# Second MLP product of an encoder block: all columns of the seven middle row chunks in seven products, 512-column matmuls, weight differences on GpSimd

## The chip, the cores and the metric

The kernel runs on one core of a Trainium2 chip. The metric is the device time of one execution in microseconds, taken as the median of several runs. The engines are TensorE (PE in the profile, its weight loads PEld), VectorE (DVE), ScalarE (ACT), GpSimd (POOL) and SyncE (SP), which issues most DMAs. Sources are written L12 for line 12 of the kernel.

## The reference

One pre-norm transformer layer on 512 tokens of width 2048, all in float32. The attention parts are not touched here. What matters is the end:

```python
x = x + mixed @ w_out[l]
h = rms_norm(x, mlp_norm_g[l])
x = x + jnp.square(jax.nn.relu(h @ w_ff1[l])) @ w_ff2[l]      # d_ff = 8192
return rms_norm(x, final_norm_g)
```

The second MLP product is a 512 x 8192 matrix F (the squared ReLU) times w_ff2, 8192 x 2048.

## The kernel before

Every float32 product is made of three passes in a rounded float32 format: an operand is split into a high part (a cast on ScalarE, L89) and a low part (the difference, on VectorE, L90), and the product takes high x high, high x low and low x high. `split` does this for a tile of 128 x 1024 elements, `unit` loads such a tile of weights and splits it into one of four `hi` and four `lo` buffers (the raw load goes through one of three `raw` buffers).

The rows of w_ff2 are taken in nine chunks: 512, seven times 1024, 512. F comes from the first product, which stores each piece of 256 columns to DRAM (`f_d`) with the row sums and differences s1 to s4 that a Strassen step needs (`s_d`). The second product adds into `SF`, a float32 tile in SBUF (two halves of the tokens, four column groups of 512).

The first chunk is a plain product (`plain`): for each of four column groups, 48 matmuls of 512 columns; ScalarE copies the result into SF. A middle chunk does three quarters of the columns in Strassen form and the last quarter plain. `spair` is one Strassen pair: it takes 512 columns as two halves of 256, and makes seven products (`sprod`, L949 to L951) of 2 x 4 x 3 = 24 matmuls of 256 columns each. The products are, in order, a11, a12, s2, s1, s3, s4 and a22, each against one weight block or one sum of weight blocks. Those weight differences are four VectorE subtractions a pair:

```python
TT(b11, b12, b11, ALU.subtract)
TT(t2, b22, b11, ALU.subtract)
TT(b12, b22, b12, ALU.subtract)
TT(t2, b21, t2, ALU.subtract)
```

After each product the PSUM tile is added into SF by VectorE (`sacc`, through the helper at L187). The weights for this are a copy of w_ff2 packed in units of 256 columns, `w_ff2s`. The plain quarter takes 96 matmuls of 512 columns and four additions into SF.

The operands of chunk c+1, four tiles of F and four of sums, are loaded and split during the plain quarter of chunk c; F alternates between two pools, the sums have one set of buffers. The last chunk (512 rows) is plain again and runs together with the residual sum and the final norm (`f2l`).

The order on each engine and on each DMA queue is not that of the text: a planner orders the instructions by their place in the text and by when it expects their operands and buffers, and every engine then runs its list in order. GpSimd has no work in the second product; elsewhere it adds masks (L437) and sums (L492).

Of the kernel before, what the change touches and what calls it, by code (L numbers as in the profile page):

```python
# [17 lines left out]
P = 128  # L18
# [13 lines left out]
NSP = 3  # L32
# [5 lines left out]
def block_kernel(ctx, tc, x, xT, w_c, w_ckv, w_qkv, w_uqn, w_uqr, w_ukv, rpb, gcols, w_out, w_ff1, w_ff2, w_ff2s, g_fin,  # L38
# [88 lines left out]
    # ---------------------------------------------------------------- input norm, latents  # L127
# [123 lines left out]
    # ---------------------------------------------------------------- neighbourhood projections  # L251
# [30 lines left out]
    def strassen_t(nm, getA, b, m1, tile, v, t2):  # L282
        """v[nh][:, token half] = (A B)^T for 256 columns of B given as four blocks."""
# [122 lines left out]
    # ---------------------------------------------------------------- neighbourhood attention  # L406
# [103 lines left out]
    # ---------------------------------------------------------------- attention operands  # L510
# [69 lines left out]
    # ---------------------------------------------------------------- latent attention  # L580
# [88 lines left out]
    # ---------------------------------------------------------------- output projection  # L669
# [174 lines left out]
    def ff1_pair(i):  # L844
# [10 lines left out]
        nc.scalar.dma_start(out=f_d[c][q], in_=vt)  # L855
        if strassen(c):
# [7 lines left out]
            nc.sync.dma_start(out=s_d[c][q], in_=st)  # L864
# [17 lines left out]

    def load_f(c, q):
        if q == 0:
            F[c] = []
        name = f"fa{c}_{q}"
        if c % 2 == 0:
            t = iot(name)
        else:
            t = [fpool.tile([P, UNIT], F32R, name=f"{name}_{j}", tag=f"f{j}", bufs=4) for j in range(2)]  # L890
        if c == 0:
            raw = raw_unit(f_d[c][q], name)
        else:
            raw = fsp.tile([P, UNIT], F32, name=name + "r", tag="fr", bufs=2)
            nc.sync.dma_start(out=raw, in_=f_d[c][q])
        split(t[0], t[1], raw)
        F[c].append([v.rearrange("p (b n) -> p b n", b=4) for v in t])

    def load_s(c, q):
        if q == 0:  # L900
            SS[c] = []
        raw = fsp.tile([P, UNIT], F32, name=f"sr{c}_{q}", tag="fr", bufs=2)
        nc.sync.dma_start(out=raw, in_=s_d[c][q])
        t = [fsp.tile([P, UNIT], F32R, name=f"fs{c}_{q}_{j}", tag=f"fs{q}{j}", bufs=1) for j in range(2)]
        split(t[0], t[1], raw)
        SS[c].append([v.rearrange("p (b n) -> p b n", b=4) for v in t])
# [6 lines left out]
    nf2 = [0]  # L913

    def f2t(name):
        i = nf2[0] % 8
        nf2[0] += 1
        return mmt(name) if i < 4 else (sct, sct, trt, pvt)[i - 4](name)

    def half(ap):  # L920
        return ap.rearrange("p (b n) -> p b n", b=2)

    def plain(c, n, k0, hook):
        ps = [f2t(f"f2_{c}_{n}_{m}") for m in range(NM)]
        ng = CH[c] // 256
        for g in range(ng):
            u = unit(w_ff2[k0 // 256 + g, n], 2, f"w2_{c}_{n}_{g}")
            hook()
            for j in range(2):
                k = 2 * g + j  # L930
                for m in range(NM):
                    mm3(ps[m], fk(c, k, m), pair(u, j, slice(0, 512)), k == 0, k == 2 * ng - 1)
        for m in range(NM):
            if c == 0:
                nc.scalar.copy(sf(m, n), half(ps[m]))
            else:
                TT(sf(m, n), half(ps[m]), sf(m, n), ALU.add)

    BLK = {"a11": 0, "a21": 1, "a12": 2, "a22": 3, "s1": 0, "s2": 1, "s3": 2, "s4": 3}

    def sprod(ps, c, a, b, first):
        kw = dict(skip_group_check=True)
        src = (F if a[0] == "a" else SS)[c]
        for mm in range(2):
            o = ps[:, mm, :]
            for kk in range(4):
                ah, al = (t[:, BLK[a], mm * P:(mm + 1) * P] for t in src[kk])
                bh, bl = (t[:, kk] for t in b)
                nc.tensor.matmul(o, ah, bh, start=first and kk == 0 and mm == 0, stop=False, **kw)  # L949
                nc.tensor.matmul(o, ah, bl, start=False, stop=False, **kw)  # L950
                nc.tensor.matmul(o, al, bh, start=False, stop=kk == 3, **kw)  # L951

    def sacc(ps, th, nb):
        TT(SF[th][:, nb], ps, SF[th][:, nb], ALU.add)

    def spair(c, j, hook):
        nm = f"{c}_{j}"
        kg = 2 * (c - 1)

        def ld(kh, nh):  # L960
            src = w_ff2s[kg + kh, 2 * j + nh]
            if nh == 0:
                return raw_unit(src, f"sb{kh}0_{nm}")
            b = fsp.tile([P, UNIT], F32, name=f"sb{kh}1_{nm}", tag=f"sb{kh}1", bufs=2)
            nc.sync.dma_start(out=b, in_=src)
            return b

        def opS(k, src):
            u = unit_bufs(f"{k}_{nm}")
            split(u[0], u[1], src)  # L970
            return [t.rearrange("p (k n) -> p k n", k=4) for t in u]

        b11, b21, b12, b22 = ld(0, 0), ld(1, 0), ld(0, 1), ld(1, 1)
        PX, PY, PZ = (half(f2t(f"s{x}{nm}")) for x in "xyz")
        t2 = fsp.tile([P, UNIT], F32, name=f"st2_{nm}", tag="st2", bufs=1)
# [181 lines left out]
```

## Time and profile before

| | |
|---|---|
| median of 3 runs | 2032.79 us (2027.8 to 2033.24) |
| span of the profiled execution, first to last instruction | 2028.5 us |
| TensorE busy | 1999.8 us, 99% of the span |
| VectorE busy | 1530.3 us, 75% |
| ScalarE busy | 991.2 us, 49% |
| GpSimd busy | 63.6 us, 3% |
| DMA moved | 307.66 MB, mean 152 GB/s |
| granted TensorE clock, mean | 0.997 |

The profiled execution has no run time of its own on record beside its span; the median of the runs lies 4.3 us above that span. Matmuls are pipelined, so the length that a matmul shows (0.39 us for 512 columns, 0.28 for 256) is longer than the distance to the next; the distance between starts is what counts. The first product ends and the second begins at 1350 us of the span.

### The profile page before, as it was taken

The numbers are of one execution on the slowest core, as the hardware profiler recorded it, in microseconds if no ns is written. First come the engines' busy times: TensorE is split into PE (matmuls) and PEld (weight loads), VectorE is DVE, ScalarE is ACT, GpSimd is POOL, SyncE is SP. The second block draws the span as 40 slices with busy tenths as digits, with TensorE's granted clock in tenths as the row PEclk, the third lists the DMA queues.
The fourth block names the chain that finished last, engine by engine and source line by source line (L and its number), as shares of the span: only waits on it lengthen the run. The fifth ranks groups of instructions, "written<-read, shape, count | busy, mean of one in ns | idle before, by whom it ended". The sixth has DMA issues, their size and how long they took to land. (4 is left out here: it accounts for less than half of the span.)

```text
span 2028.5 us, 34883 instructions
## 1 busy us (share of the span) xinstructions
PE 1999.8 (99%) x14388; PEld 1876.9 (93%) x14388; DVE 1530.3 (75%) x1927; ACT 991.2 (49%) x1429; POOL 63.6 (3%) x73
## 2 busy tenths in 40 slices
PE   8999999999999999999999999999999999999998
PEld 7999999877887899999999999998999999999996
DVE  8787777777435787777878787757888887878776
ACT  5644454565314565555555555555434344444333
POOL 2000010100000000000000000000000000000000
PEclk9999999999999999999999999999999999999999
DMA  8454454431334344445353444456435354453352
GB/s 278 134 182 164 154 166 131 133 99 53 94 124 156 123 162 153 169 144 184 129 187 138 175 154 159 164 166 211 161 131 178 124 170 152 133 200 127 103 207 94
DMA packets 97999, 307.66 MB, mean 152 GB/s; under 512 B 10800, under 2 KB 16688, under 8 KB 97584
## 3 DMA queue, kind: packets, MB, share of 16 engines
q1 hardware_dynamic: 87136, 274.76, 40.5%
q10 hardware_dynamic: 9936, 29.52, 3.7%
q8 instruction: 113, 1.85, 0.4%
q0 software_dynamic: 768, 1.15, 0.2%
q14 instruction: 46, 0.38, 0.1%
HBM read 254.27 MB, written 52.26 MB: 151 GB/s over the span
## 5 line engine op out<-in xcount | busy, mean ns | idle before, releaser
L187 DVE TENSOR_TENSOR SF<-sx,SF 128x512 f32<-128x512 f32 x84 | 57.6, 686 | 16.2 <-PE sx L951 16.1
L90 DVE TENSOR_TENSOR fs<-sr,fs 128x1024 fp32r<-128x1024 f32 x28 | 34.2, 1223 | 20.4 <-ACT fs L89 20.4
L125 POOL TENSOR_TENSOR stat<-stat,nhalf 128x1 f32<-128x1 f32 (+1 forms) x6 | 4.4, 730 | 1409.2 <-DVE stat L124 1409.2
L89 ACT CAST fs<-sr 128x1024 fp32r<-128x1024 f32 x28 | 28.8, 1049 | 27.0 <-DMA sr<-s_d 23.3
L853 ACT ACTIVATE v<-v 128x512 f32<-128x512 f32 x64 | 40.4, 632 | 2.0
L852 ACT ACTIVATE v<-v 128x512 f32<-128x512 f32 x64 | 40.3, 630 | 1.0
L187 DVE TENSOR_TENSOR b<-b,b 128x1024 f32<-128x1024 f32 x32 | 38.9, 1216 | 0.0
L187 DVE TENSOR_TENSOR SF<-sz,SF 128x512 f32<-128x512 f32 x42 | 28.9, 687 | 11.7 <-PE sz L951 11.7
L949 PE MATMUL sx<-st_0hi,fs 128*128 128x256 f32 x112 | 32.8, 292 | 4.4 <-ACT sb_0hi L89 4.4
L99 PE MATMUL f<-w_0hi,fa 128*128 128x512 f32 x88 | 34.4, 390 | 0.0
L100 PE MATMUL f<-w_0lo,fa 128*128 128x512 f32 x88 | 34.3, 390 | 0.0
L101 PE MATMUL f<-w_0hi,fa 128*128 128x512 f32 x88 | 34.2, 389 | 0.0
L99 PE MATMUL f<-w_1hi,fa 128*128 128x512 f32 x88 | 34.2, 389 | 0.0
L100 PE MATMUL f<-w_1lo,fa 128*128 128x512 f32 x88 | 34.2, 389 | 0.0
L101 PE MATMUL f<-w_1hi,fa 128*128 128x512 f32 x88 | 34.2, 389 | 0.0
L90 DVE TENSOR_TENSOR mpt<-mt,mpt 128x512 fp32r<-128x512 f32 x32 | 22.0, 686 | 14.2 <-ACT mpt L89 14.2
L950 PE MATMUL sx<-st_0lo,fs 128*128 128x256 f32 x112 | 32.5, 291 | 0.0
L951 PE MATMUL sx<-st_0hi,fs 128*128 128x256 f32 x112 | 32.5, 290 | 0.0
L949 PE MATMUL sx<-st_1hi,fs 128*128 128x256 f32 x112 | 31.7, 283 | 0.0
L950 PE MATMUL sx<-st_1lo,fs 128*128 128x256 f32 x112 | 31.7, 283 | 0.0
L951 PE MATMUL sx<-st_1hi,fs 128*128 128x256 f32 x112 | 31.7, 283 | 0.0
L949 PE MATMUL sx<-st_2hi,fs 128*128 128x256 f32 x112 | 31.7, 283 | 0.0
(2952 smaller groups left out, 8954.6 us busy)
## 6 DMA issues: line engine op xcount, KB each, us to landing
b<-in_w_ff_dram SPq DMA_DIRECT2D x64, 512.0 KB, 5.9
sb<-in_w_ff2s_dram SPq DMA_DIRECT2D x42, 512.0 KB, 4.3
f_d<-v ACTq DMA_DIRECT2D x32, 512.0 KB, 7.2
s_d<-sv SPq DMA_DIRECT2D x28, 512.0 KB, 6.9
sr<-s_d SPq DMA_DIRECT2D x28, 512.0 KB, 4.6
nb<-in_w_qkv_dram SPq DMA_DIRECT2D x24, 512.0 KB, 4.6
sb_0r<-in_w_ff2s_dram SPq DMA_DIRECT2D x14, 512.0 KB, 5.2
sb_1r<-in_w_ff2s_dram SPq DMA_DIRECT2D x14, 512.0 KB, 4.6
```

Of the source, the lines that this page charges most:

```text
L89: i = nc.scalar.copy(hi, src)
L90: nc.vector.tensor_tensor(out=lo, in0=src, in1=hi.bitcast(F32), op=ALU.subtract)
L99: nc.tensor.matmul(ps, ah, bh, start=first, stop=False)
L100: nc.tensor.matmul(ps, ah, bl, start=False, stop=False)
L101: nc.tensor.matmul(ps, al, bh, start=False, stop=last)
L125: nc.gpsimd.tensor_tensor(out=dst, in0=dst, in1=nhalf[:, :cnt], op=ALU.pow)
L187: nc.vector.tensor_tensor(out=out, in0=a, in1=b, op=op)
L852: nc.scalar.activation(v[h], v[h], AF.Relu)
L853: nc.scalar.activation(v[h], v[h], AF.Square)
L949: nc.tensor.matmul(o, ah, bh, start=first and kk == 0 and mm == 0, stop=False, **kw)
L950: nc.tensor.matmul(o, ah, bl, start=False, stop=False, **kw)
L951: nc.tensor.matmul(o, al, bh, start=False, stop=kk == 3, **kw)
```

## The change

The seven middle chunks are done in Strassen form over all columns. A pair now takes 1024 columns as two halves of 512, so a chunk is two pairs, each product is 24 matmuls of 512 columns, and the plain quarter and the packed copy `w_ff2s` go. The weight blocks are two units of 1024 elements each, with loads of their own; a product splits them one unit at a time into the same four hi/lo buffers. The differences (now eight of 1024 elements a pair) are issued on GpSimd. The products accumulate in PSUM tiles of two banks (`ps_w`, four of them), and an addition into SF covers 1024 elements. F and its sums are stored to DRAM by block, so that one load brings one operand of a chunk; the seven operands of the next chunk are refilled one at a time, each after its last product in the second pair, into the single buffer it had (`load_op`; the buffers are those that held the first product's operands, pool `ops1`, which stays open). The operands of the first middle chunk are loaded ahead of the plain first chunk. The tail's residual tiles and last weights use operand buffers too.

```diff
-NSP = 3
...
+    def raw_unit(src, name, k=0):
+        raw = wp.tile([P, UNIT], F32, name=name + "r", tag="raw", bufs=3)
+        if k:
+            raw = raw.rearrange("p (k n) -> p k n", k=k)
...
-    f_d = [[tc.dram_tile([P, UNIT], F32, name=f"f_d{c}_{q}") for q in range(CH[c] // 256)] for c in range(NC_)]
-    s_d = [[tc.dram_tile([P, UNIT], F32, name=f"s_d{c}_{q}") for q in range(CH[c] // 256)] for c in range(NC_)]
+    f_d, s_d = ([tc.dram_tile([P, 4, CH[c] // 256, 256], F32, name=f"{t}_d{c}") for c in range(NC_)] for t in "fs")
...
-        nc.scalar.dma_start(out=f_d[c][q], in_=vt)
+        nc.scalar.dma_start(out=f_d[c][:, :, q, :], in_=vt.rearrange("p (b n) -> p b n", b=4))
...
+    ps_w = open_pool("ps_w", space=PSUM)
+    fb = open_pool("fb", side="left")
...
+    def load_op(c, nm):
+        raw = raw_unit((f_d if nm[0] == "a" else s_d)[c][:, BLK[nm]], f"fo{c}_{nm}", 4)
+        t = op_tiles(nm, 0, f"fo{c}_{nm}")
+        split(t[0], t[1], raw)
+        FO[c, nm] = t
...
+    def spair(c, j, k0, hook):
         nm = f"{c}_{j}"
-        kg = 2 * (c - 1)
...
+        def ld(kh, nh, u):
+            pool, tag, bufs = ((iop, "io0", 4), (iop, "io1", 4), (fb, "b12", 2), (fb, "b22", 2))[2 * nh + kh]
+            t = pool.tile([P, UNIT], F32, name=f"sb{kh}{nh}_{nm}_{u}", tag=tag, bufs=bufs)
+            nc.sync.dma_start(out=t, in_=w_ff2[k0 // 256 + kh * nu + u, 2 * j + nh])
+            return t
+
+        b11, b21, b12, b22 = ([ld(kh, nh, u) for u in range(nu)] for nh in range(2) for kh in range(2))
+        t2 = [fb.tile([P, UNIT], F32, name=f"st2_{nm}_{u}", tag="t2", bufs=2) for u in range(nu)]
+        PX, PY, PZ = (wide(f"s{x}{nm}") for x in "xyz")
+
+        def prod(ps, a, src, first):
+            for u in range(nu):
+                b = unit_bufs(f"{a}_{nm}_{u}")
+                split(b[0], b[1], src[u])
+                b = [t.rearrange("p (k n) -> p k n", k=2) for t in b]
+                for mm in range(2):
+                    for k2 in range(2):
+                        kk = 2 * u + k2
+                        ah, al = (t[:, kk, mm * P:(mm + 1) * P] for t in FO[c, a])
+                        bh, bl = (t[:, k2] for t in b)
+                        kw = dict(skip_group_check=True)
+                        nc.tensor.matmul(ps[:, mm], ah, bh, start=first and kk == 0, stop=False, **kw)
+                        nc.tensor.matmul(ps[:, mm], ah, bl, start=False, stop=False, **kw)
+                        nc.tensor.matmul(ps[:, mm], al, bh, start=False, stop=kk == 2 * nu - 1, **kw)
+            hook(a)
+
+        def acc(ps, th, n):
+            TT(SF[th][:, n], ps, SF[th][:, n], ALU.add)
+
+        def GT(out, a, b):
+            for u in range(nu):
+                nc.gpsimd.tensor_tensor(out=out[u], in0=a[u], in1=b[u], op=ALU.subtract)
+
+        prod(PX, "a11", b11, True)
+        for u in range(nu):
+            nc.gpsimd.tensor_tensor(out=b11[u], in0=b12[u], in1=b11[u], op=ALU.subtract)
+            nc.gpsimd.tensor_tensor(out=t2[u], in0=b22[u], in1=b11[u], op=ALU.subtract)
+        GT(b12, b22, b12)
+        acc(PX, 0, n1)
+        prod(PY, "a12", b21, True)
+        acc(PY, 0, n1)
+        prod(PX, "s2", t2, False)
+        GT(t2, b21, t2)
+        acc(PX, 0, n2)
+        prod(PZ, "s1", b11, True)
+        acc(PZ, 1, n2)
+        prod(PX, "s3", b12, False)
+        acc(PX, 1, n2)
+        prod(PZ, "s4", b22, False)
+        acc(PZ, 0, n2)
+        prod(PX, "a22", t2, False)
+        acc(PX, 1, n1)
...
+    for nm in ORDER:
+        load_op(1, nm)
+    for n in range(4):
+        plain(0, n, 0)
+    k0 = CH[0]
+    for c in range(1, NC_ - 1):
+        spair(c, 0, k0, lambda a: None)
+        if c + 1 < NC_ - 1:
+            spair(c, 1, k0, lambda a, c=c: load_op(c + 1, a))
...
+        for h, t in enumerate(op_tiles(("a11", "s1", "s3", "s4")[m], 0, f"xf{m}")):
```

## Rows read from the trace of the kernel before

**Rows 1.** The page, first line and part 1: busy us (share of span) xinstructions.

```profile
span 2028.5 us, 34883 instructions
...
PE 1999.8 (99%) x14388; PEld 1876.9 (93%) x14388; DVE 1530.3 (75%) x1927; ACT 991.2 (49%) x1429; POOL 63.6 (3%) x73
```

**Rows 2.** Windows: length, busy us per engine, PEclk granted, DMA share, GB/s.

```profile
1400.00:1410.00 10.00, 5.97 (x34) 6.00 (x35) 6.61 (x7) 4.84 (x6) 0.00 (x0) 0.66 0.80 258
...
1543.10:1625.40 82.30, 82.30 (x602) 78.54 (x601) 68.67 (x72) 34.16 (x33) 0.00 (x0) 1.00 0.47 154
```

**Rows 3.** Waits of PE from 1310 us: waiter, releaser, total us, times, longest.

```profile
PE sx L949 <- ACT sb_0hi L89: 4.4, 1, 4.4
```

**Rows 4.** Timeline of PE around one middle chunk: start us, us, instruction.

```profile
1542.97 0.40 PE L99 MATMUL f<-w_0hi,fa 128*128 128x512 f32 x1
...
1564.76 0.28 PE L949 MATMUL sx<-sb_0hi,fa 128*128 128x256 f32 x1
...
1625.23 0.40 PE L99 MATMUL f<-w_0hi,fa 128*128 128x512 f32 x1
```

**Rows 5.** Groups of instructions in that chunk: xcount, busy us, mean ns.

```profile
L187 DVE TENSOR_TENSOR SF<-sx,SF 128x512 f32<-128x512 f32 x12 | 8.2, 686 | 1.9 <-PE sx L951 1.9
L90 DVE TENSOR_TENSOR fs<-sr,fs 128x1024 fp32r<-128x1024 f32 x5 | 6.1, 1221 | 2.4 <-ACT fs L89 2.4
...
L89 ACT CAST fs<-sr 128x1024 fp32r<-128x1024 f32 x4 | 4.1, 1048 | 3.5 <-DMA sr<-s_d 2.8 <-PE sz L950 0.6
```

**Rows 6.** Timeline of DVE, two low parts and an SF addition.

```profile
1486.92 1.22 DVE L90 TENSOR_TENSOR st_0lo<-sb,st_0hi 128x1024 fp32r<-128x1024 f32 x1
1488.06 1.22 DVE L90 TENSOR_TENSOR fa<-fa_3r,fa 128x1024 fp32r<-128x1024 f32 x1
1489.19 0.68 DVE L187 TENSOR_TENSOR SF<-sy,SF 128x512 f32<-128x512 f32 x1
```

**Rows 7.** Timeline of POOL and DVE where both work.

```profile
113.94 1.85 POOL L437 TENSOR_TENSOR bm<-bm,bt 128x768 f32<-128x768 f32 x1 [5.04 <-DMA bm<-in_mask_dram]
...
114.03 2.84 DVE L90 TENSOR_TENSOR ob_00lo<-nb,ob_00hi 128x1024 fp32r<-128x1024 f32 x1 [1.59 <-ACT ob_00hi L89]
...
259.75 3.48 POOL L437 TENSOR_TENSOR bm<-bm,bt 128x768 f32<-128x768 f32 x1 [34.72 <-DMA bm<-in_mask_dram]
...
260.29 1.22 DVE L187 TENSOR_TENSOR nb<-nb,nb 128x1024 f32<-128x1024 f32 x1
...
261.43 0.42 DVE L187 TENSOR_TENSOR nv<-pz,nu 128x256 f32<-128x256 f32 x1
...
267.68 1.29 POOL L492 TENSOR_TENSOR ssn<-ssn,nsq 128x512 f32<-128x512 f32 x1 [4.46 <-ACT nsq L491]
...
267.93 2.13 DVE L187 TENSOR_TENSOR nv<-nv,rho 128x1024 f32<-128x1024 f32 x1
```

**Rows 8.** Groups of POOL: xcount, busy us, mean ns, idle before.

```profile
L437 POOL TENSOR_TENSOR bm<-bm,bt 128x768 f32<-128x768 f32 x8 | 21.1, 2641 | 220.4 <-DMA bm<-in_mask_dram 190.3 <-DVE wr1lo L90 18.1 <-DVE qrn L567 12.0
```

**Rows 9.** DMA issues: xcount, KB each, median us to landing.

```profile
w_0r<-in_w_ff_dram SPq DMA_DIRECT2D x11, 512.0 KB, 4.4
```

**Rows 10.** Timeline of SP, ACT and PE into the second product.

```profile
1331.73 0.33 SPq L74 DMA_DIRECT2D w_0r<-in_w_ff_dram  x1
...
1341.74 1.05 ACT L89 CAST w_0hi<-w_0r 128x1024 fp32r<-128x1024 f32 x1 [1.51 <-PE pz L290]
...
1350.14 0.40 PE L99 MATMUL f<-w_0hi,fa 128*128 128x512 f32 x1
```

**Rows 11.** Timeline of PE in the first Strassen pair.

```profile
1399.34 0.28 PE L951 MATMUL sy<-sb_0hi,fa 128*128 128x256 f32 x1
1404.03 0.55 PE L949 MATMUL sx<-st_0hi,fs 128*128 128x256 f32 x1 [4.41 <-ACT sb_0hi L89]
...
1408.41 0.28 PE L951 MATMUL sx<-st_0hi,fs 128*128 128x256 f32 x1
```

**Rows 12.** Waits of ACT: waiter, releaser, total us, times, longest.

```profile
ACT st_1hi L89 <- PE sx L951: 33.2, 21, 1.8
```

More of the change, by code (lines that the diff above doesn't have):

```diff
@@ L869, in block_kernel, with wide, op_tiles @@
     close_pool("vp")
-    close_pool("ops1")
-    fpool = open_pool("fpool", side="left")
-    fsp = open_pool("fsp", side="left")
+    close_pool("ps_ax")
+    close_pool("ps_mm")
+    ps_w = open_pool("ps_w", space=PSUM)
+    fb = open_pool("fb", side="left")
     sfp = open_pool("sfp", side="right")
-    SF = [sfp.tile([P, 8, 2, 256], F32, name=f"SF{th}") for th in range(2)]
+    SF = [sfp.tile([P, 4, 2, 512], F32, name=f"SF{th}") for th in (1, 0)][::-1]
     def sf(m, n):
-        return SF[m // 2][:, 2 * n:2 * n + 2, m % 2, :]
-    F, SS = {}, {}
-    def load_f(c, q):
[L884 to L895, printed above, removed]
-        split(t[0], t[1], raw)
[L897 to L906, printed above, removed]
+        return SF[m // 2][:, n, m % 2, :]
+    def wide(name):
+        return ps_w.tile([P, 2, 512], F32, name=name, tag="w", bufs=4)
+    def op_tiles(nm, g, name):
+        return [ops1.tile([P, 4, 256], F32R, name=f"{name}_{j}", tag=f"{nm}_{g}_{j}") for j in range(2)]
+    BLK = {"a11": 0, "a21": 1, "a12": 2, "a22": 3, "s1": 0, "s2": 1, "s3": 2, "s4": 3}
+    ORDER = ("a11", "a12", "s2", "s1", "s3", "s4", "a22")
+    FO, F = {}, {}
+    def load_f(c, q):
+        raw = raw_unit(f_d[c][:, :, q, :], f"fa{c}_{q}", 4)
+        t = op_tiles(("a11", "s3")[q], 1, f"fa{c}_{q}")
+        split(t[0], t[1], raw)
+        F.setdefault(c, []).append(t)
     def fk(c, k, m):
@@ L911, in fk, with plain @@
         return tuple(x[:, b, m % 2 * P:(m % 2 + 1) * P] for x in F[c][k % nk])
[L913 to L924, printed above, removed]
+    def load_op(c, nm):
[3 more added lines that the diff above has]
+        FO[c, nm] = t
+    def plain(c, n, k0):
+        ps = [wide(f"f2_{c}_{n}_{th}") for th in range(2)]
         ng = CH[c] // 256
@@ L931, in plain @@
                 for m in range(NM):
[L932 to L951, printed above, removed]
@@ L953, in sacc @@
-    def sacc(ps, th, nb):
-        TT(SF[th][:, nb], ps, SF[th][:, nb], ALU.add)
-    def spair(c, j, hook):
-        nm = f"{c}_{j}"
-        kg = 2 * (c - 1)
[L960 to L975, printed above, removed]
-        n1, n2 = 2 * j, 2 * j + 1
-        sprod(PX, c, "a11", opS("sb11", b11), True)
-        sacc(PX, 0, n1)
-        sprod(PY, c, "a12", opS("sb21", b21), True)
-        sacc(PY, 0, n1)
-        TT(b11, b12, b11, ALU.subtract)
-        TT(t2, b22, b11, ALU.subtract)
-        hook()
-        sprod(PX, c, "s2", opS("st2", t2), False)
-        sacc(PX, 0, n2)
-        sprod(PZ, c, "s1", opS("st1", b11), True)
-        sacc(PZ, 1, n2)
-        TT(b12, b22, b12, ALU.subtract)
-        sprod(PX, c, "s3", opS("st3", b12), False)
-        sacc(PX, 1, n2)
-        hook()
-        sprod(PZ, c, "s4", opS("sb22", b22), False)
-        sacc(PZ, 0, n2)
-        TT(t2, b21, t2, ALU.subtract)
-        sprod(PX, c, "a22", opS("st4", t2), False)
-        sacc(PX, 1, n1)
@@ L1043, in block_kernel @@
             raw = raw_unit(src, f"wl{n}_{g}")
[L1044 to L1053 removed]
+            if n == 1:
+                u = [iop.tile([P, UNIT], F32R, name=f"wl{n}_{g}_{j}", tag=f"io{j}", bufs=4) for j in range(2)]
+            else:
+                u = [t.rearrange("p k n -> p (k n)") for t in op_tiles(("a12", "s2")[g], 0, f"wl{n}_{g}")]
+            split(u[0], u[1], raw)
+            us[n, g] = [t.rearrange("p (k n) -> p k n", k=2) for t in u]
     def add_sf(m, xs):
         for n in range(4):
[L1057 to L1060 removed]
+            nc.vector.scalar_tensor_tensor(out=xs[n], in0=sf(m, n), scalar=stat[:, R2 + m:R2 + m + 1],
+                                           in1=xs[n], op0=ALU.mult, op1=ALU.add)
+    xfs += [load_x1(m) for m in range(1, NM)]
     add_sf(0, xfs[0])
```

77 lines of the change are left out of this document (29 added, 48 removed).

## Prediction

> **What bounds the kernel now.** The page's first part, then the windows by stage, then TensorE's waits and its timeline at the seams. TensorE is busy for 99% of the span [rows 1] and a whole middle chunk runs without a gap at full granted clock [rows 2]; in the second product and what follows it waits once for any length, 4.4 us [rows 3]. So time is matmul starts times their spacing. The timeline gives the spacing: from the first 512-column matmul of a chunk's plain quarter to the first of its Strassen pairs are 96 matmuls in 1564.76 - 1542.97 = 21.79 us, 227 ns each; from there to the next chunk's plain quarter are 3 x 168 = 504 matmuls of 256 columns in 60.47 us, 120 ns each [rows 4]. A chunk costs 82.26 us. VectorE is second (68.7 of 82.3 us), ScalarE is half idle, GpSimd is empty in this stage [rows 2].
>
> **TensorE's new work.** A middle chunk becomes 2 pairs x 7 products x 24 = 336 matmuls of 512 columns with the same operand roles as the plain quarter: 336 x 0.227 = 76.27 us. Against 82.26 this removes 5.99 us a chunk, 41.9 us over seven. Of it a part is columns (172,032 instead of 178,176: 6,144 x 0.443 ns = 2.7 us a chunk), the rest is that two 256-column matmuls cost 240 ns and one of 512 costs 227. The Trainium skill (TensorE: Matmul & The Clock Gate, Back-to-back issue gap) has the width divided by 2.4 GHz plus about 2.5 ns, 109 and 216 ns; by it the chunk would lose only 3.2 us, 22.7 in all. The trace does not agree: both widths cost some 11 to 13 ns more, so the narrow one pays that twice.
>
> **VectorE and GpSimd.** Now VectorE makes four weight differences a pair (1.22 us each, as the other 1024-element forms of [rows 5]); that leaves it. What stays per chunk: 28 low parts of weights and 7 of refilled operands, all reading two SBUF tiles; back to back they start 1.135 us apart [rows 6]: 35 x 1.135 = 39.7 us. Then 14 additions into SF of 1024 elements from PSUM: a 512-element one takes 0.686 us and the 1024-element forms 1.22, so I estimate the same 1.135 spacing: 15.9 us. VectorE alone would need 55.6 of 76.3 us.
>
> GpSimd gets 16 subtractions of 128x1024 a chunk. No row has that size. 512 elements took 1.29, 768 took 1.85 when alone [rows 7], so 1024 is estimated at 1.85 + 0.56 = 2.41 us: 38.6 us a chunk, affordable for GpSimd by itself. The mean of the 768 form, 2.64 us, is longer [rows 8] because it fights VectorE for something: a 1024-element subtraction of two SBUF tiles that began 0.09 us after GpSimd's took 2.84 instead of 1.22, so it was held for 1.71 us of GpSimd's 1.85; another behind the 512 form took 2.13. In reverse, GpSimd's add issued at 259.75 took 3.48: it sat through the whole of VectorE's next two-SBUF subtraction (260.29 to 261.51) and finished one own length after it. The PSUM-reading addition at 261.43 ran beside it in its normal 0.42 us [rows 7]. The rows thus say: two-SBUF work of VectorE and GpSimd's work exclude each other, PSUM-reading work is free, and back-to-back VectorE work keeps GpSimd out. The Trainium skill (SBUF — State Buffer, Who interferes with whom) states this as an exclusive lock on a shared port pair, the second fully blocked; the trace agrees, except that GpSimd was passed over although it had asked before the 260.29 subtraction.
>
> So each subtraction takes 2.41 - 0.14 = 2.27 us from VectorE, less what VectorE can do meanwhile. If GpSimd enters as an SF addition begins, that addition's 1.135 us is covered and the loss is 1.135. I walk one pair: after the first low part of a11 the eight subtractions queue up; six meet additions (the last two of the pair before, then a11, a12, s2, s1), two enter in gaps where VectorE waits for ScalarE's cast of t2 and cost it the full 2.27. Per chunk: 39.7 + 15.9 + 12 x 1.135 + 4 x 2.27 = 78.3 us, against TensorE's 76.27. The ring of four hi/lo buffers, each 12 x 0.227 = 2.72 us of matmuls (half a product), lets a low part be ready 3 x 2.72 - 1.05 - 1.22 = 5.9 us early, and evens out that the second pair carries the seven refills and the first none. I take 78.3: VectorE sets the pace by a little, 3.96 us a chunk are gained, 27.7 in all. Bounds: with nearly every addition overlapped (14 of 16) VectorE needs 76.0, TensorE leads and all 41.9 come; with none 91.9, 9.6 worse a chunk.
>
> ScalarE casts 35 x 1.05 = 37 us a chunk (1.048 each, [rows 5]), under half. Weights, 16 units, and 7 refills are 23 loads of 512 KB a chunk where there were 24; at the 47% DMA share of [rows 2] they stay hidden. b12 and b22 have one pair's buffers only, but are free after the low parts of s3 and s4 and wanted six and four half products later (16 and 11 us) for a landing time of about 4.4 [rows 9]. The f_d and s_d stores become 1 KB pieces: they lie under a 19.8 us column pair of the first product with two buffers each; no row has their price, below nothing is excluded since bytes are equal, and it takes a landing of more than two pairs to show. I take 0. POOL's queue holds nothing else here.
>
> **The seams.** (1) Into the second product. Now the first w_ff2 unit is asked for at 1331.73 and cast at 1341.74, so TensorE goes on at 1350.14 without a stop [rows 10]. After, nine loads stand before it (two of chunk 0, seven operands of chunk 1), all through three raw buffers; each is held until its op tile is free, which is when the last first-product pair has used that operand. Walking slots from 1331.73 with 4.4 us to land and 2.3 to split: s3's tile is free at about 1344.5, a22's at 1350.1, a22's load goes out near 1350 and the first weight near 1353, cast near 1358.5. TensorE would stand about 9 us and restart slowly. Low bound 0, if the weight is let past. (2) Chunk 1's third product waits 1399.46 to 1404.03 for casts and loads that all arrive together (80% DMA share), and the next twenty matmuls are 0.213 apart instead of 0.120, at the lower clock of 1.2 GHz (0.66 of full granted as the mean of that stretch): 4.4 + 1.9 = 6.3 us [rows 2, 3, 11]. The operands of chunk 1 now come before the plain products and the products are twice as long, so I expect 5 of it gone. Together I take +4 (between -6 and +11). (3) The tail keeps its 192 matmuls and its last chain; 0 to 2 us, taken 0: x_d and last weights land in op tiles, free a product or more before they are wanted.
>
> **Sum.** Profiled span 2028.5; 2028.5 - 27.7 + 4 = 2004.8. The median of the runs lies 4.3 us above that span, which I take to be what lies around it: 2009 us.
>
> **Rivals.** *A, all hidden:* GpSimd slips under the additions and idle time, TensorE sets the chunk: 2032.8 - 41.9 = 1991, 1986 if the seams help too. For it: VectorE has 20 us a chunk without GpSimd; against: the exclusion rows. *B, half overlapped, no change:* 91.9 - 1.135 x = 82.26 at x = 8.5 of 16; there the whole gain is eaten, 2033 plus seams. *C, slower:* GpSimd's back-to-back subtractions keep VectorE out as VectorE kept GpSimd out, so nothing overlaps: 2032.8 + 7 x 9.6 = 2100; it decides from fewer than eight overlaps a chunk. For it: two holds of VectorE in [rows 7]; against: four subtractions form chains through b11 and t2, so GpSimd must let go between them. By the lock as the Trainium skill words it, whoever starts first wins, which leaves C open. *D, refills in the way:* a refill's cast stands in ScalarE's and VectorE's queue waiting for its product; the order is made by a planner that has kept such waits under 2 us so far [rows 12]; each wait beyond the 5.9 us reserve is a TensorE stall.
>
> **Chances.** Forecast (1998 to 2022) 0.5; A 0.2; B with D (2022 to 2040) 0.15; C 0.15. Range 1988 to 2040: below it about 0.06, above it 0.14. The measurement tells 0.3%, 6 us, from no change: faster 0.75 (the forecast, A and a third of B), same 0.08, slower 0.17.
>
> **What would show it.** Right: 512-column s-matmuls 227 ns apart; GpSimd subtractions alone at 2.4 us, many at 3 to 4; VectorE low parts with a second group near 2.5 to 3.5 us; SF additions undisturbed; chunks 77 to 80 us, with TensorE's small waits in second pairs falling on low parts; a stop near 1350 of some 9 us and none of 4 us in chunk 1. Wrong: chunks at 76.3 (A), or above 82 with VectorE near 100% (B, C); a granted clock below full inside chunks, which would mean the stalls are long ones.

## The result, and the profile after

The change made the kernel slower: 2076.82 us median (2075.6 to 2078.34) against 2032.8, ratio 1.0223 with a 95% interval of 1.0209 to 1.0238. That is above the forecast of 2009 and above the end of its range, 1988 to 2040.

The page of after answers to [rows 1]: TensorE is busy for 1 us less in a span 47 us longer, and VectorE and GpSimd have gained work.

```profile
span 2075.9 us, 31188 instructions
...
PE 1998.7 (96%) x12540; PEld 1776.2 (86%) x12540; DVE 1608.9 (78%) x1780; ACT 1003.2 (48%) x1435; POOL 410.1 (20%) x185
```

Two middle chunks of after as windows (columns as in [rows 2]): a chunk takes 86.6 to 87.4 us where it took 82.3 (the first of the seven 81.0, the last 90.6), VectorE is busy for 81.5 to 81.8 of them (68.7 before), and the mean granted clock is below full. The third row, a window of the same trace, is a stretch around one stall: 0.50, the level of 1.2 GHz.

```profile
1493.17:1579.75 86.58, 81.22 (x337) 63.80 (x337) 81.54 (x50) 35.86 (x35) 50.34 (x17) 0.98 0.38 140
1579.75:1667.15 87.40, 82.19 (x339) 64.78 (x338) 81.83 (x50) 35.87 (x35) 50.54 (x17) 0.96 0.38 139
...
1591.10:1597.00 5.90, 4.72 (x11) 3.68 (x12) 5.90 (x4) 1.99 (x2) 4.74 (x3) 0.50 0.11 41
```

The four largest groups of TensorE's waits in the second product of after (columns as in [rows 3], where there was one of 4.4 us). All but one end with a low part that VectorE makes. The waits in `sz`, at s1 of the second pair, come back in all seven middle chunks; the one in `sy`, at a12 of the first pair, from the second of them on:

```profile
PE sy L950 <- DVE a_1lo L93: 18.0, 6, 3.4
PE f L102 <- ACT w_0hi L92: 11.9, 1, 11.9
PE sz L950 <- DVE s_1lo L93: 8.8, 7, 1.4
PE sz L950 <- DVE s_0lo L93: 4.7, 7, 3.0
```

What such a wait costs is seen in TensorE's timeline, at the second product (a12) of the first pair of chunk 3. The wait is 3.38 us, and the matmuls behind it are 0.42 us apart in place of 0.233, until about 1597.5:

```profile
1592.28 0.79 PE L950 MATMUL sy<-a_1lo,fo_a 128*128 128x512 f32 x1 [3.38 <-DVE a_1lo L93]
1592.87 0.63 PE L951 MATMUL sy<-a_1hi,fo_a 128*128 128x512 f32 x1
1593.29 0.63 PE L949 MATMUL sy<-a_1hi,fo_a 128*128 128x512 f32 x1
```

VectorE's timeline ahead of that stall, to be read beside GpSimd's:

```profile
1575.24 1.21 DVE L190 TENSOR_TENSOR SF<-sz,SF 128x1024 f32<-128x1024 f32 x1
1576.37 2.52 DVE L93 TENSOR_TENSOR fo_s<-fo_s4r,fo_s 128x1024 fp32r<-128x1024 f32 x1
1578.81 3.42 DVE L93 TENSOR_TENSOR a_1lo<-sb,a_1hi 128x1024 fp32r<-128x1024 f32 x1
1582.16 3.43 DVE L93 TENSOR_TENSOR a_0lo<-sb,a_0hi 128x1024 fp32r<-128x1024 f32 x1
1585.52 1.21 DVE L190 TENSOR_TENSOR SF<-sx,SF 128x1024 f32<-128x1024 f32 x1
1586.65 2.29 DVE L93 TENSOR_TENSOR fo_a<-fo_a22r,fo_a 128x1024 fp32r<-128x1024 f32 x1
1588.87 3.35 DVE L93 TENSOR_TENSOR a_1lo<-sb,a_1hi 128x1024 fp32r<-128x1024 f32 x1
```

```profile
1575.39 2.42 POOL L963 TENSOR_TENSOR sb<-sb,sb 128x1024 f32<-128x1024 f32 x1 [17.04 <-DVE a_0lo L93]
1577.88 3.27 POOL L964 TENSOR_TENSOR st<-sb,sb 128x1024 f32<-128x1024 f32 x1
1581.12 3.40 POOL L959 TENSOR_TENSOR sb<-sb,sb 128x1024 f32<-128x1024 f32 x1
1584.46 3.41 POOL L963 TENSOR_TENSOR sb<-sb,sb 128x1024 f32<-128x1024 f32 x1
1587.94 3.20 POOL L964 TENSOR_TENSOR st<-sb,sb 128x1024 f32<-128x1024 f32 x1
```

The two engines take turns. GpSimd's subtraction of 1575.39 begins while VectorE reads PSUM and takes 2.42 us; from then on every low part of a weight on VectorE (1.22 alone) takes 3.4, because it first sits through one subtraction, and each subtraction then sits through one low part. The two refills here (`fo_s`, `fo_a`) take 2.3 to 2.5, since part of the subtraction that they wait for has run during the addition before them. From 1575.24 to 1592.22 it finished seven instructions, which 1.135 us apart would be 7.9 us, in 17.0: 9.1 us late in a stretch in which TensorE needs a new low part every 2.8 us.

The seam shows in TensorE's timeline, last matmul of the first product and first of the second, and in SP's, where the first w_ff2 unit is asked for at 1360.61; in [rows 10] it was at 1331.73.

```profile
1353.68 0.28 PE L294 MATMUL px<-a,ot_31lo 128*128 128x256 f32 x1
1365.87 1.22 PE L102 MATMUL f<-w_0hi,fa 128*128 128x512 f32 x2 [11.91 <-ACT w_0hi L92]
```

```profile
1358.26 0.32 SPq L74 DMA_DIRECT2D fo_a22r<-f_d  x1
1360.61 0.33 SPq L77 DMA_DIRECT2D w_0r<-in_w_ff_dram  x1
```

By stage the 47.4 us of span are: up to the end of the first product 3.7, the seam about 14 with its slow restart, the plain chunk 1.3, the middle chunks 605.9 (1412.49 to 2018.39) against 582.4 (1393.71 to 1976.06), so 23.5, and the tail 5.1. Of the 3.7, 3.2 stand already ahead of the first product, which begins at 712.3 us where it began at 709.1: in attention code that the change does not touch. Over all fourteen traces of this document that start lies between 709.1 and 713.4. The first product itself takes 641.4 against 640.9, a column pair 19.83 before and after, so the stores of 1 KB pieces cost nothing. The middle chunks were to become 7 x 78.3 = 548.

### The profile page after: what moved, and what is told of

The parts are those of the page before. It is cut to its first block, busy times and chain, and to the rows that moved or that the text cites. A ratio compares the mean times of both kernels' runs of the same rounds, so it can differ in the third digit from the quotient of the medians.

```text
span 2075.9 us, 31188 instructions
## 1 busy us (share of the span) xinstructions
PE 1998.7 (96%) x12540; PEld 1776.2 (86%) x12540; DVE 1608.9 (78%) x1780; ACT 1003.2 (48%) x1435; POOL 410.1 (20%) x185
## 5 line engine op out<-in xcount | busy, mean ns | idle before, releaser
L963 POOL TENSOR_TENSOR sb<-sb,sb 128x1024 f32<-128x1024 f32 x28 | 80.2, 2864 | 979.9 <-DVE a_0lo L93 978.7
L959 POOL TENSOR_TENSOR sb<-sb,sb 128x1024 f32<-128x1024 f32 x28 | 91.9, 3282 | 0.0
L964 POOL TENSOR_TENSOR st<-sb,sb 128x1024 f32<-128x1024 f32 x28 | 90.4, 3228 | 2.2
L959 POOL TENSOR_TENSOR st<-sb,st 128x1024 f32<-128x1024 f32 x28 | 85.7, 3072 | 20.5 <-DVE s_0lo L93 12.3
L93 DVE TENSOR_TENSOR a_1lo<-sb,a_1hi 128x1024 fp32r<-128x1024 f32 x28 | 74.7, 2668 | 9.8 <-ACT a_1hi L92 9.8
L93 DVE TENSOR_TENSOR a_0lo<-sb,a_0hi 128x1024 fp32r<-128x1024 f32 x28 | 57.4, 2049 | 21.3 <-ACT a_0hi L92 21.3
L190 DVE TENSOR_TENSOR SF<-sx,SF 128x1024 f32<-128x1024 f32 x56 | 67.9, 1213 | 3.7 <-PE sx L951 3.6
L93 DVE TENSOR_TENSOR s_0lo<-sb,s_0hi 128x1024 fp32r<-128x1024 f32 x42 | 65.8, 1566 | 3.3 <-ACT s_0hi L92 3.3
L93 DVE TENSOR_TENSOR s_1lo<-sb,s_1hi 128x1024 fp32r<-128x1024 f32 x42 | 56.3, 1340 | 0.0
L950 PE MATMUL sz<-s_0lo,fo_s 128*128 128x512 f32 x112 | 45.0, 402 | 4.7 <-DVE s_0lo L93 4.7
L92 ACT CAST s_1hi<-st 128x1024 fp32r<-128x1024 f32 x14 | 14.7, 1050 | 69.7 <-POOL st L964 68.0
L949 PE MATMUL sx<-s_0hi,fo_s 128*128 128x512 f32 x112 | 45.2, 403 | 1.3 <-DVE SF L190 1.3
```

Source lines behind the costliest of these rows:

```text
L92: i = nc.scalar.copy(hi, src)
L93: nc.vector.tensor_tensor(out=lo, in0=src, in1=hi.bitcast(F32), op=ALU.subtract)
L190: nc.vector.tensor_tensor(out=out, in0=a, in1=b, op=op)
L949: nc.tensor.matmul(ps[:, mm], ah, bh, start=first and kk == 0, stop=False, **kw)
L950: nc.tensor.matmul(ps[:, mm], ah, bl, start=False, stop=False, **kw)
L959: nc.gpsimd.tensor_tensor(out=out[u], in0=a[u], in1=b[u], op=ALU.subtract)
```

## The experiments

Three theories for the chunks came up in turn. L: the turns of VectorE and GpSimd make the low parts late. P: the planner put the differences ahead of more urgent work. R: the seven refills in the second pair put too much on VectorE there. The seam was a question of its own, and so was a thing that no forecast had: every 512-column matmul of the second product is 233.3 ns from the next, where the kernel before had 227. Experiments 2 to 9 and 11 are one run each; since the traces differ by up to 4 us ahead of the first product, small differences are read from stages and not from the whole time.

**1. All differences on VectorE, places unchanged.**

```diff
-                nc.gpsimd.tensor_tensor(out=out[u], in0=a[u], in1=b[u], op=ALU.subtract)
+                nc.vector.tensor_tensor(out=out[u], in0=a[u], in1=b[u], op=ALU.subtract)
```

and the same for those of b11 and t2.

> The changed kernel with all eight weight differences of a pair back on VectorE; nothing else differs. Theory L (GpSimd and VectorE exclude each other, so each subtraction of 2.27 us is taken from VectorE): VectorE then needs 39.7 + 15.9 + 16 x 1.135 = 73.8 us a chunk, less than the 336 x 0.2333 = 78.4 that TensorE needs; TensorE's waits of some 8 us a chunk go, a chunk takes 78.4 to 79.5, the time falls from 2077 to 2017 to 2025, some 8 to 16 us below the kernel before. Rival R (the singly refilled operands stand in the queues of ScalarE and VectorE): the waits stay, above all in the second pair of a chunk, and the chunk stays above 82 us, the time above 2045.

2052.77 us (four runs; ratio to before 1.0098, 1.0081 to 1.0115). 24 us of the loss go with GpSimd, and that leaves a chunk of 84.5 us where VectorE is busy for only 74.2 (the profiled execution is the slowest of the four, 2059.4; at the median a chunk is up to 1 us shorter). VectorE's timeline at the boundary of two chunks shows why:

```profile
1570.90 1.22 DVE L93 TENSOR_TENSOR a_1lo<-sb,a_1hi 128x1024 fp32r<-128x1024 f32 x1
1572.03 1.22 DVE L964 TENSOR_TENSOR st<-sb,sb 128x1024 f32<-128x1024 f32 x1
1573.17 1.22 DVE L963 TENSOR_TENSOR sb<-sb,sb 128x1024 f32<-128x1024 f32 x1
1574.40 1.23 DVE L93 TENSOR_TENSOR fo_a<-fo_a22r,fo_a 128x1024 fp32r<-128x1024 f32 x1
1575.54 1.22 DVE L190 TENSOR_TENSOR SF<-sx,SF 128x1024 f32<-128x1024 f32 x1
1576.67 1.22 DVE L964 TENSOR_TENSOR st<-sb,sb 128x1024 f32<-128x1024 f32 x1
1577.81 2.35 DVE L959 TENSOR_TENSOR sb<-sb,sb 128x1024 f32<-128x1024 f32 x2
1580.08 1.22 DVE L190 TENSOR_TENSOR SF<-sx,SF 128x1024 f32<-128x1024 f32 x1
1581.21 1.22 DVE L93 TENSOR_TENSOR a_0lo<-sb,a_0hi 128x1024 fp32r<-128x1024 f32 x1
```

Between the low parts of a11 and a12 stand five differences, a refill and two additions. TensorE waits 2.10 us for the addition of 1580.08, because the planner has put the first matmul of s2, into the same sum, ahead of a12's, and 0.27 us more for the low part of 1581.21; the lower clock does the rest:

```profile
1581.44 0.77 PE L949 MATMUL sx<-s_0hi,fo_s 128*128 128x512 f32 x1 [2.10 <-DVE SF L190]
1582.48 0.80 PE L950 MATMUL sy<-a_0lo,fo_a 128*128 128x512 f32 x1 [0.27 <-DVE a_0lo L93]
```

So L alone falls short of the forecast; P or R remained.

**2. GpSimd's work kept, its results not used.** The subtractions go into t2, and the products use the unsubtracted blocks.

```diff
-            nc.gpsimd.tensor_tensor(out=b11[u], in0=b12[u], in1=b11[u], op=ALU.subtract)
+            nc.gpsimd.tensor_tensor(out=t2[u], in0=b12[u], in1=b11[u], op=ALU.subtract)
...
-        prod(PX, "s2", t2, False)
+        prod(PX, "s2", b22, False)
```

> The changed kernel in which GpSimd does its eight subtractions a pair, but writes them to a scratch tile that nobody reads; the products take unsubtracted weight blocks instead, so the sums of the Strassen step are left out of the result. Nobody waits for GpSimd's results any more, but it still reads SBUF next to VectorE. Theory L: VectorE is still held for about 2.25 us by most of the 16 subtractions; chunks stay at 84 to 88 us (86.6 in the changed kernel), low parts next to GpSimd's work still take 3.4 us. Rival T (the delay is the chain of eight subtractions, t2 and b11 come too late): chunks fall to 78.4 us, the time to about 2020.

One run, 2055.24 us; a middle chunk 83.3, with VectorE busy for 79.3. Theory L had 84 to 88 and T 78.4. Nobody waits for GpSimd's results, and still the chunk is 4.9 us over TensorE's own 78.4 (336 x 233.3 ns): the turns do that without any late result. By difference, late results have the other 3 to 4 us. But in the middle chunks TensorE waits at a11 and a12 of the first pair, behind a refilled second pair, and nowhere else (in the last one also at the start of its second pair), and the first, ahead of which no refill runs, takes 78.4 with all its turns. So it takes the refills beside the turns to do this harm.

**3. Part of the differences on VectorE.** The expectation miscounts: the edit moved four of a pair's eight differences (b11 and t2) to VectorE and left four (b12 and the last t2).

```diff
-            nc.gpsimd.tensor_tensor(out=b11[u], in0=b12[u], in1=b11[u], op=ALU.subtract)
+            nc.vector.tensor_tensor(out=b11[u], in0=b12[u], in1=b11[u], op=ALU.subtract)
```

and the same for t2 in the line behind it.

> The changed kernel with the first six differences of a pair (b11, t2 and b12) on VectorE and only the last two (t2 for a22) on GpSimd. Theory L: of 16 subtractions a chunk 4 still hold VectorE for 2.25 us: 39.7 + 15.9 + 12 x 1.135 + 4 x 2.25 = 78.2 us of VectorE against 78.4 of TensorE, less what the additions cover: chunk 78.4 to 80, time 2020 to 2030. Rival T (late chain): the same 78.4, since the chain's urgent part is gone. Read from it: how many us one subtraction on GpSimd costs VectorE, 1.1 more than on VectorE by theory L.

One run, 2037.56 us, above what both theories had said (2020 to 2030); a middle chunk 82.3 (one of them 80.8), with one wait of 2.1 us at a12 of the first pair. Chunk 1, before which no refill runs, took 78.4. That spoke for R.

**4. The operand loads behind the plain quarters.**

```diff
-    for nm in ORDER:
-        load_op(1, nm)
     for n in range(4):
         plain(0, n, 0)
+        for nm in ORDER[2 * n:2 * n + 2]:
+            load_op(1, nm)
```

> The changed kernel with the loads of the first middle chunk's seven operands placed two at a time behind each quarter of the plain first chunk instead of ahead of all of it. Theory Q (nine loads through three raw buffers stand ahead of the first weight): TensorE's wait of 12 us before the first 512-column matmul, and about 2 us of the lower clock after it, go to 0 to 2 us; the time falls by 11 to 14 us, to 2063 to 2066. Rival: the PSUM or SBUF space that the stage takes over is released late, and the wait stays within 3 us of 12.

2065.58 us, 11.2 less. The wait ahead of the second product falls from 11.9 to 2.7 us and is no longer one for the weight; the chunks are as in the changed kernel. The loads ahead of the first weight were the cause.

```profile
PE f L102 <- ACT v L852: 2.7, 1, 2.7
```

**5. All differences on VectorE, where the kernel before issued them.**

```diff
         prod(PY, "a12", b21, True)
         acc(PY, 0, n1)
+        DT(b11, b12, b11)
+        DT(t2, b22, b11)
         prod(PX, "s2", t2, False)
...
         acc(PZ, 1, n2)
+        DT(b12, b22, b12)
         prod(PX, "s3", b12, False)
```

and the last t2 behind the sums of s4.

> Changed kernel with all 16 differences of a chunk on VectorE and each issued where the kernel before issued it: the first two kinds behind the sums of a12, the third behind those of s1, the last behind those of s4. In the version where all of them stood right behind a11's product a chunk took 84.5 us (time 2052.8). Theory P (there six differences in a row, put ahead of the low parts that TensorE waits for, made the stall at a pair's start; VectorE's sum of 75 us a chunk would fit): no wait over 0.5 us inside the chunks, 78.4 to 80 us a chunk, time 2052.8 - 7 x 4.5 to 6.1 = 2010 to 2021. Theory R (the seven operand refills inside the second pair put about 8 us too much on VectorE just there, wherever the differences stand): a wait of 2 us stays at each first pair, 82.5 to 84.5 us a chunk, time 2039 to 2053.

2022.27 us, 1 us above the range of P. P holds all the same: no wait in any middle chunk, and 78.5 us for one, in windows of which VectorE is busy for 74.8. R by itself is refuted, since the refills are all there:

```profile
1561.17:1639.69 78.52, 78.52 (x337) 63.04 (x336) 74.80 (x66) 36.01 (x36) 0.00 (x0) 1.00 0.46 153
```

**6. The changed kernel without refills.**

```diff
-            spair(c, 1, k0, lambda a, c=c: load_op(c + 1, a))
+            spair(c, 1, k0, lambda a, c=c: FO.update({(c + 1, a): FO[c, a]}))
```

> Changed kernel without the refills of chunks 2 to 7: the seven products of these chunks go on with the operands of chunk 1 (42 loads with their casts and low parts are left out, and the output is that of chunk 1's operands). Theory L (VectorE and GpSimd taking turns, 3.4 us for each low part beside a subtraction, is the whole of it): the subtractions meet the same low parts, the waits at a12 and at s2/s1 stay, 84 to 87 us a chunk, time 2058 to 2077. Theory R (the refills' 7 low parts of 1.14 us or, beside a subtraction, 3.4 us, leave VectorE late at the boundary of two chunks): the wait at the first pair's a12 goes, chunks 2 to 7 fall to the 81.0 us of chunk 1 or less, down to 78.4, time 2076.8 - 6 x 5.6 to 8.2 = 2028 to 2043.

2032.53 us. A middle chunk takes 79.35 with GpSimd's sixteen subtractions all there:

```profile
1566.56:1645.91 79.35, 78.94 (x337) 62.92 (x336) 68.20 (x42) 29.07 (x28) 49.44 (x17) 1.00 0.29 106
```

So the turns without refills cost a chunk 0.9 us, the refills without GpSimd (5) cost nothing, and both together 8 to 9. Neither theory was it alone: each eats the same reserve. The last middle chunk, where loads of the last chunk still stand, is dearer here too: 84.4, against 90.6 in the changed kernel.

**7. Spacing: place of the stationary operand, kind of PSUM tile.**

```diff
-        t = op_tiles(("a11", "s3")[q], 1, f"fa{c}_{q}")
+        t = [v.rearrange("p (k n) -> p k n", k=4) for v in iot(f"fa{c}_{q}")]
...
-            ps = pw[:, n % 2]
+            ps = ps_w.tile([P, 512], F32, name=f"f2l_{m}_{n}", tag="w", bufs=4)
```

The first edit is for chunk 0 alone.

> Changed kernel in which the stationary operands of the plain chunk 0 lie in the buffers where the kernel before had them (left side), everything else there as in the changed kernel, and in which the last chunk's sums stand in tiles of one 512-column bank in place of two-bank tiles, its operands as in the changed kernel. The spacing of the 512-column matmuls is 233 ns in all stages of the changed kernel's second product and 227 in the kernel before. Theory O (place of the stationary operand): chunk 0 back at 227, the last chunk stays at 233. Theory B (two-bank sums): chunk 0 stays at 233, the last chunk back at 227. Neither: 233 in both. Time in all cases within 3 us of 2076.8.

Theory O. TensorE's timelines in chunk 0 and in the last chunk: nine matmuls take 2.04 us (227 each) in the first and 2.10 (233) in the second.

```profile
1400.04 0.39 PE L102 MATMUL f<-w_0hi,fa 128*128 128x512 f32 x1
...
1402.08 0.39 PE L102 MATMUL f<-w_1hi,fa 128*128 128x512 f32 x1
```

```profile
2030.04 0.39 PE L102 MATMUL f2l<-wl,fa 128*128 128x512 f32 x1
...
2032.14 0.39 PE L102 MATMUL f2l<-wl_1hi,fa 128*128 128x512 f32 x1
```

The time, 2069.46, fell by more than expected, since chunk 0's operands now wait for other buffers: the seam's wait was 5.7 us in place of 11.9.

**8. Parts 4 and 5 together.**

> The version of the kernel with all differences on VectorE at the places of the kernel before, and the loads of chunk 1's seven operands taken behind the quarters of plain chunk 0, two at a time, in place of ahead of it. If the two parts simply add: 11 us less than the version without the moved loads, so 1999 to 2010 by theory P, 2028 to 2042 by theory R. If the moved loads take VectorE's time from chunk 1, some of the 11 us comes back there.

2011.24 us, 11.0 less than 5 (and so, as 5 was, 1 us above the forecast): the two add. 78.5 us a chunk, no wait in one.

**9 and 10. 32 bytes at the right edge of SBUF.** In the program's memory map the stationary operands stood 32 bytes past a multiple of 64; an unused tile moves them to one.

```diff
+    open_pool("pad", side="right").tile([P, 8], F32, name="pad")
     ops1 = open_pool("ops1", side="right")
```

> Changed kernel with one unused tile of 32 bytes a partition put at the right edge of SBUF, so that everything on that side moves down by 32 bytes and nothing else changes. The stationary operands of the second product, which lie there, began 32 bytes past a multiple of 64; now they begin at one, as those of chunk 0 did in the run where they lay on the left. Theory M (it was the 32 bytes): every 512-column matmul of the second product at 227 ns in place of 233, chunks shorter by up to 336 x 6.6 ns = 2.2 us where TensorE sets the pace and by less where the late low parts do; time 2076.8 - 4 to 18 = 2059 to 2073. Theory S (it is the side of SBUF, or the distance to the moving operand): 233 stays in all stages, time 2073 to 2078.

> The version with all differences on VectorE at the places of the kernel before and with the loads of chunk 1's operands behind the quarters of plain chunk 0 (2011.2 in its run), and the unused tile of 32 bytes at the right edge of SBUF. Theory M: 7 x 336 + 2 x 192 matmuls, 6.6 ns less each, 18 us: 1993 to 1996, a chunk 76.3 us; VectorE has 75 us of work in one, so if it then sets the pace, some wait of up to 1 us a chunk comes back, 2000. Theory S: 2011.

2077.42 us on the changed kernel, 2016.16 (2012.73 to 2017.12, five runs; ratio to before 0.9921, 0.9907 to 0.9934) on the version of 8. The spacing is 230 to 235 in both, 233 on the mean (a chunk of 10 takes 78.2 to 78.5). Theory M falls. The 32 bytes were not free elsewhere: in both runs a column pair of the first product, 168 matmuls of 256 columns, takes 19.95 us in place of 19.83, 3.8 us over its 32 pairs.

**11. Differences on GpSimd, at the places of 5.** The edit of 5 with `nc.gpsimd`.

> Changed kernel with the differences left on GpSimd, issued where the kernel before issued them (behind the sums of a12, s1 and s4), so that with the versions on VectorE at either place all four cases of engine and place are there: GpSimd early 2076.8, VectorE early 2052.8, VectorE late 2022.3. Theory of the turns (each subtraction holds VectorE some 2.3 us, and its result comes 2.4 to 3.4 us after its operands wherever it stands): the taking turns costs the same 4 to 8 us a chunk and the results come later than in the changed kernel, s2's four subtractions (13 us in turns) standing between a12's low part and s2's: chunks of 90 to 105 us, time 2100 to 2200. Theory of the place (the planner's order alone made the stalls): chunks near 78.4, time 2022 to 2035.

2076.65 us: neither forecast. It is the changed kernel again: in the middle chunks up to the sixth the waits agree in place and to 0.02 us in length. On GpSimd the place in the text decides nothing: its queue holds only these subtractions, and the first of a pair starts behind the same low part in both. On VectorE it decides 30 us, since other work stands in that queue.

**12. The operands in the lower part of SBUF.** The version of 8, with two sets of buffers exchanged: the seven products' operands go into `iop` and `fb`, the weight blocks and differences into `ops1`. The first part of the edit; the tail's tiles also take other buffers of `ops1`:

```diff
-        t = op_tiles(nm, 0, f"fo{c}_{nm}")
+        i = ORDER.index(nm)
+        if i < 4:
+            t = [v.rearrange("p (k n) -> p k n", k=4) for v in iot(f"fo{c}_{nm}")]
+        else:
+            t = [fb.tile([P, 4, 256], F32R, name=f"fo{c}_{nm}_{j}", tag=f"{nm}_{j}", bufs=1) for j in range(2)]
```

> The version with all differences on VectorE at the places of the kernel before and with the loads of chunk 1's operands behind the quarters of plain chunk 0 (2011.2 in its run), and two sets of 14 buffers exchanged: the stationary operands of the seven products now lie in the lower part of a partition (64 to 122 KB), where those of chunk 0 lay in the run that read 227 ns there, and the weight blocks and their differences in the upper part (156 to 229 KB). The operands of chunk 0 and of the last chunk stay in the upper part as a control. Theory S (a stationary operand in the upper part makes a 512-column matmul 233 ns): 227 in the pairs and 233 still in chunk 0 and the last chunk; 7 x 336 x 6.6 ns = 15.5 us less, 1996, or up to 2003 if VectorE, with 75 us of work to a chunk of 76.3, makes TensorE wait at times. If what counted in chunk 0 was something else about its buffers (their shape, how they rotate): 233 in the pairs too, 2011 to 2016.

1991.98 us (1989.72 to 1993.45, five runs), ratio to before 0.9799 (0.9785 to 0.9812): 2% faster than the kernel before. Theory S. Nine matmuls of a pair take 2.04 us, nine of chunk 0 in the same run 2.09 (timeline, chunk 0 first):

```profile
1384.82 0.39 PE L102 MATMUL f<-w_1hi,fa 128*128 128x512 f32 x1
...
1386.91 0.39 PE L102 MATMUL f<-w_1hi,fa 128*128 128x512 f32 x1
...
1599.66 0.39 PE L957 MATMUL sy<-a_1lo,fo_a 128*128 128x512 f32 x1
...
1601.70 0.39 PE L957 MATMUL sy<-a_1lo,fo_a 128*128 128x512 f32 x1
```

The time is 4 us under the forecast because the tail is shorter too, 56 us against 60 in 8. A chunk is 76.5 us, with TensorE busy throughout and VectorE close behind:

```profile
1552.88:1629.36 76.48, 76.45 (x338) 63.05 (x336) 74.48 (x66) 35.87 (x36) 0.00 (x0) 1.00 0.46 158
```

The versions that bear on the chunks in one table (a middle chunk, its VectorE time, the whole):

| differences | refills | chunk us | VectorE us | time us |
|---|---|---|---|---|
| GpSimd (the change; 11 alike) | yes | 86.6 to 87.4 | 81.5 to 81.8 | 2076.8 |
| GpSimd, results unused (2) | yes | 83.3 | 79.3 to 79.8 | 2055.2 |
| four of eight on GpSimd (3) | yes | 82.3, one 80.8 | 75.1 to 76.0 | 2037.6 |
| GpSimd (6) | no | 79.35 | 68.2 | 2032.5 |
| VectorE, early (1) | yes | 84.5 | 74.2 | 2052.8 (this profile 2059.4) |
| VectorE, late (5) | yes | 78.5 | 74.8 | 2022.3 |
| as 5, seam mended (8; with pad, 10) | yes | 78.5; 78.4 | 74.8; 74.9 | 2011.2; 2016.2 |
| as 8, operands low (12) | yes | 76.5 | 74.5 | 1992.0 |
| GpSimd, seam mended (4) | yes | 86.6 to 87.4 | 81.5 to 81.6 | 2065.6 |

## Why the prediction was wrong, step by step

**TensorE's new work: right in kind, 2.1 us a chunk short, and hidden.** 336 matmuls at 227 ns are 76.27 us; 12 has 76.5. In the changed kernel they are 233.3 ns apart, 78.4 a chunk, which the stalls of VectorE cover. (The "11 to 13 ns" that the prediction finds on top of both widths are 11 for each.) "The same operand roles as the plain quarter" was not enough: their place in SBUF had moved too, and 7 and 12 show that this makes the difference.

**The step that failed: "VectorE sets the pace by a little", 78.3 us a chunk.** It has two faults. First the overlap. I read "back-to-back VectorE work keeps GpSimd out" from one case in [rows 7], and counted on 12 of 16 subtractions to meet an SF addition. The engines take turns instead. VectorE's 81.6 busy us, less 55.6 of its own, are 26.0 for sixteen subtractions; by the step's own prices (2.27, less 1.135 for each that is covered) that is 9 covered, not 12, and 3.3 us a chunk. (The Trainium skill, SBUF — State Buffer, Who interferes with whom, has a VectorE instruction with two SBUF inputs contend with GpSimd's reads; the 3.4 us of a low part agree, and the order of turns is this trace's.) The alone price, 2.41 us, was right: 2.42 and 2.38.

The second fault is larger. A chunk's sum was compared with a chunk's time, as if VectorE's work could lie anywhere in it. With 81.6 of 87 us VectorE still idles 5 us a chunk while TensorE waits for it elsewhere: six of a pair's eight subtractions come in one row, at the boundary of two pairs, just where the last two refills stand. The two timelines above give the account. a12's second low part was ready at 1592.22; TensorE could have used it from about 1588.9. The two refills there (fo_s, fo_a) took 4.81 us; without them it would have been in time, and in 6 it is. The reserve of 5.9 us, which was to even this out, was worked out for the refills alone. D's mechanism and B's price met in one place, and I gave them 0.15.

**What a stall costs.** Waits were counted at their length. A wait of 3.4 us brought some 2.3 us more at the lower clock (the 24 matmuls of that a12 are 479 ns apart on the mean, 23 x 0.246 = 5.7); over a chunk, 5 us of waits made 8 to 9. I had used that price in the seam, from [rows 11], and not here. Not every wait has it. Behind the waits of 1.4 us in the second pairs of after, the matmuls go on 0.233 us apart, at a granted clock of 1.00:

```profile
1560.62 0.50 PE L950 MATMUL sz<-s_1lo,fo_s 128*128 128x512 f32 x1 [1.41 <-DVE s_1lo L93]
1560.96 0.40 PE L951 MATMUL sz<-s_1hi,fo_s 128*128 128x512 f32 x1
1561.19 0.40 PE L949 MATMUL sz<-s_1hi,fo_s 128*128 128x512 f32 x1
```

In 3 the same wait of 2.1 us came out both ways in neighbouring chunks (windows as above): 2.4 us over the 78.4 with the clock at 1.00, 3.9 us with 0.98.

```profile
1568.82:1649.58 80.76, 78.66 (x338) 63.02 (x337) 76.04 (x58) 36.09 (x36) 23.67 (x8) 1.00 0.43 150
1649.58:1731.86 82.28, 80.21 (x337) 64.17 (x336) 75.09 (x58) 36.11 (x36) 23.67 (x8) 0.98 0.43 147
```

**The change on GpSimd at all.** The forecast took the subtractions' removal from VectorE as given and weighed only the lock. All on VectorE, at their old places, would have been 39.7 + 15.9 + 16 x 1.135 = 73.8 us by the forecast's own rows, under TensorE's 76.3, without any lock: 5 and 12 measured 74.5 to 74.8. Rival A's time, 1991, was reached in that way, not by overlap.

**The seams.** (1) Right in mechanism, short in size: 12 us and 2 of restart, where 9 was said; SP asked for the weight at 1360.6, not 1353, and 4 removes 11. (2) The bubble in chunk 1 is gone, as expected. (3) The tail was taken at 0 and cost 5.1 us (57.5 against 52.4), 3.2 of it two waits for the residual sums on VectorE; in 8 it is longer still, 60 us against 52. Why was not tried. The 3.7 us up to the end of the first product are, but for 0.5, a later start of it, which varies by 4 us over the traces. f_d and s_d at 0: right, with landings of 6.8 and 6.6 us against 7.2 and 6.9.

**C's place.** Rival C (2100) was nearer in time but not in kind: with no overlap VectorE would need 91.9 us, and it needed 81.6.

The sum of misses, on the forecast span of 2004.8: chunks 605.9 - 548.1 = 57.8, less 1.3 of the bubble that was left in the forecast; seam and plain chunk 15.3 - 9 = 6.3; start 3.7; tail 5.1: 71.6, where the spans differ by 71.1.

## What to carry to other kernels

Moving two-operand SBUF work from a full VectorE to an idle GpSimd does not take it off VectorE (81.6 us a chunk here, against 74.8 with all of it on VectorE): read what a low part costs while the other engine runs, and ask first whether the work fits where it was. A sum over a loop body is only a bound; walk the most crowded stretch, here the boundary of two pairs, with every item that stands in that queue, and price each stall with its slow restart. Where a chain of instructions shares a queue with urgent work, its place in the text is a cost of its own: 30 us here on VectorE, nothing on GpSimd.

## What the runs showed of the hardware that was not expected

A 512-column float32r matmul takes 227 ns to the next when its stationary operand lies in the lower part of a partition (64 to 122 thousand bytes in 7 and 12, up to 130 in the kernel before) and 233 when it lies at 156 to 229, with moving operand and PSUM tile of the same kind (places by the program's memory map). 32 bytes of offset do not change that (9). Nor is it the distance to the moving operand alone: in the last chunk of the changed kernel the first column group has its moving operand up there too, and its matmuls are about 231 apart, not 227. At 256 columns the place does not show: in the kernel before, those with the stationary operand at 64 to 130 thousand (`fa`) and at 138 to 171 (`fs`) are all 120 ns apart. Where between 130 and 156 it turns for 512 columns, and why, is open. Over seven chunks it is worth 14.7 us (549.8 in 8, 535.2 in 12), and the time fell by 19.

VectorE and GpSimd alternate instruction by instruction when both have two-operand SBUF work ready: 3.4 us for a subtraction of 1.22, while the additions that read PSUM stay at 1.21.
